# Small matmul groups of the mixers as pieces between contraction blocks: a hybrid pool and HGRN2 layer on one core

## Chip, cores and metric

One core of a Trainium2 chip. The time is that of one execution of the kernel in device microseconds (us); lower is better. Before the change it was run three times.

## What is computed

One layer over 2,048 tokens of width 1,024, in float32, cut to what matters:

```
mod = silu(c) @ ada_w + ada_b                       # shift, scale, gate
h   = rms_norm(x, w_pre) * (1 + scale) + shift
z   = h @ w_in                                      # 1024 -> 6144: u, g (pool), q, f_pre, v, g_h (HGRN2)
pool = trailing mean over 2/4/8/16 tokens minus token, @ pool_w, * scale, * silu(g)
f = lb + (1 - lb) * sigmoid(f_pre);  k = 1 - f      # per head of 128 channels, 8 heads
o_t = q_t @ S_t;  S_t = diag(f_t) S_{t-1} + k_t v_t^T
out = x + gate * rms_norm(concat(pool, rms_norm(o) * silu(g_h)) @ w_out)
```

## The kernel before

The tokens run in two halves of 1,024, each as two blocks of 512 (`BLK`). A **step** is one 2x2 block product by the seven-product scheme of Winograd (`quad`): seven calls of `product` (L351), each four contraction blocks of three 128x512 matmuls (L353, the operands split in a high and a low part), so 84 **products** of 128x512 a step into the three banks `ps_mm`. A head `hd` has three steps: `fq` (forget gate and query), `pool` (one of eight pool columns) and `hv` (gate and value); the list `steps` sets their order. The first half of the tokens has 24 steps and so has the second; then 16 more products, eight for each half of the contraction, make the output projection.

Weights: in the first half `granule` loads a step's columns (`wraw<-w_in`), forms sums on POOL (L324 to L333), splits each of seven operands on ACT (`w<-wraw`, L129) and DVE (L130), and stores them (`wsd<-w`, SP's queue); the second half reads them back.

Beside the products runs the **mixer** of each head, for each block of 512 tokens:

- `attn_unit`: builds the decayed attention of chunks of 128 tokens level by level. `sums` (L574) gives the diagonal and its neighbour; then for m = 2, 4, 8, 16 sixteen matmuls of 32x16 (L614), then those of 32 (L625) and of 64 (L635). After each level `place` copies the result under a mask (DVE, L594) and `update(m)` multiplies the query tile `qk` by a decay (DVE, L606, 128x512). The next level's matmuls read that tile: a chain of six groups with five links for each block and head, 160 links in all.
- `out_unit`: transposes of value and key (L653, L666) with ACT copies `v` and `kd`, outer products `kv` (L671), the chain over four chunks (L679, L681, with DVE's state update L682), squares on ACT (L688), the root on POOL (L111, L112), the scaling on DVE (L690), a transpose (L693), the gate (L694) and a store.

Other side work: `second_sums(i)` (L432 to L457) normalises 128 tokens of the second half, transposes them (L443), writes four tiles `hc` on ACT (L123) and four `hs` on POOL and stores them (`hsd`); `hc` and `hs` have one buffer each. `out_sums` (L712 to L719) loads a part of `w_out` into the tile `x`, scales it on ACT (L713), forms sums on POOL and stores them; `gate_row` makes the output gate.

The code is written step after step and a list scheduler in the framework orders each engine's instructions by a simulated time; what is written earlier has the higher priority. Each engine, and SP's queue, then runs its own list in order. Before the change the main loop wrote a whole step, and behind it the whole mixer part: `attn_unit` of block 0, then of block 1, behind `fq`; `out_unit` of block 0, then of block 1, behind `hv`.

Of the kernel before, what the change touches and what calls it, by code (L numbers as in the profile page):

```python
# [44 lines left out]
def build(nc, tc, a):  # L45
# [6 lines left out]
    with tc.tile_pool(name="dram", bufs=1, space=DRAM) as dram, \  # L52
# [295 lines left out]

        def product(ps, w, s, start):
# [76 lines left out]
        def second_sums(i):  # L426
# [8 lines left out]
            nc.scalar.activation(junk, xt, AF.Square, accum_out=ss)  # L435
            rstd_of(ss, 1, 1.0 / D)
            nc.vector.tensor_scalar(xt, xt, ss, None, ALU.mult)
            for k4 in range(0, KH, 2):
# [5 lines left out]
                for k in range(2):  # L444
# [11 lines left out]
                    for j, t_ in ((0, hc), (4, hs)):  # L456
                        nc.sync.dma_start(hsd[j:j + 4, :, k4 + k, i * n:(i + 1) * n].rearrange("j p t -> p j t"), t_)  # L457

# [9 lines left out]
        def gate_row():  # L468

            gn = wsp.tile([P, D], F32, name="gn", tag="x1", bufs=1)  # L470
            for j in range(KB):
                for n in range(2):
                    ns = slice(n * BLK, (n + 1) * BLK)
                    t_ = short("adag", "junk")
                    nc.sync.dma_start(t_, ada_w[:, j, 2 * D + n * BLK:2 * D + (n + 1) * BLK])
                    if j == 0:
                        nc.vector.tensor_scalar(gn[:, ns], t_, sc[:, 0:1], None, ALU.mult)
                    else:
                        nc.vector.scalar_tensor_tensor(gn[:, ns], t_, sc[:, j:j + 1], gn[:, ns], ALU.mult, ALU.add)
            for n in range(4):  # L480
# [8 lines left out]
                nc.sync.dma_start(gnrow[:, ns], b_)  # L489

# [72 lines left out]
        def attn_unit(hd, b, qk, tm):  # L563
# [18 lines left out]
            sums(w0, 0)  # L582
            nc.vector.tensor_tensor(Q, Q, f, ALU.mult)
            Qp, Kp = (t_.rearrange("p (n two) -> p n two", two=2) for t_ in (Q, K))
            w1 = short("w1", "w0", 2, n=BLK // 2)
            nc.gpsimd.tensor_tensor(w1, Qp[:, :, 1], Kp[:, :, 0], ALU.mult)
            sums(w1, 1)
# [20 lines left out]
            update(1)  # L608
            for m in (2, 4, 8, 16):
# [8 lines left out]
            for q in range(4):  # L618
                qs = slice(q * 32, (q + 1) * 32)
                nc.scalar.copy(attn[qs, :, qs], diag[qs])  # L620
            ps = bank("lv", (P, NC_, 32))
            for c in range(NC_):
                for q in (0, 2):
                    t = c * C + q * 32
                    nc.tensor.matmul(ps[q * 32:(q + 1) * 32, c], K[:, t:t + 32], Q[:, t + 32:t + 64],  # L625
                                     start=True, stop=True)
            for q in (0, 2):
                eng = nc.vector.tensor_copy if q else nc.scalar.copy
                qs = slice(q * 32, (q + 1) * 32)
                eng(attn[qs, :, (q + 1) * 32:(q + 2) * 32], ps[qs])  # L630
            update(32)
            ps = bank("lv", (P, NC_, 64))
            for c in range(NC_):
                t = c * C
                nc.tensor.matmul(ps[0:64, c], K[:, t:t + 64], Q[:, t + 64:t + 128], start=True, stop=True)  # L635
            nc.scalar.copy(attn[0:64, :, 64:128], ps[0:64])
            update(64)
            return attn, qk, tm[C]

        def hv_step(W):  # L640
# [5 lines left out]
            for b in range(2):  # L646
                pre = gx if b else X
                g = short("g", "g", 2, pool=ws)
                nc.scalar.activation(g, pre, AF.Sigmoid)
                nc.vector.tensor_tensor(g, pre, g, ALU.mult)  # L650
                ps = bank("tp", (P, NC_, P))
                for c in range(NC_):
                    nc.tensor.transpose(ps[:, c], vc[b][:, c * C:(c + 1) * C], ident)  # L653
                v = ws.tile([P, NC_, P], F32, name="v", tag="v", bufs=2)
                nc.scalar.copy(v, ps)
                r.append((v, g))
            return r

        def out_unit(hd, t0, attn, qk, td, v, g):

            first = t0 == 0
            Q, K = qk[:, 0], qk[:, 1]

            ps = bank("tp", (P, NC_, P))
            for c in range(NC_):
                nc.tensor.transpose(ps[:, c], K[:, c * C:(c + 1) * C], ident)  # L666
            kd = ws.tile([P, NC_, P], F32, name="kd", tag="kd", bufs=1)
            nc.scalar.copy(kd, ps)
            kv = bank("kv", (P, NC_, P))
            for c in range(NC_):  # L670
                nc.tensor.matmul(kv[:, c], kd[:, c], v[:, c], start=True, stop=True)  # L671
            sx = ws.tile([P, NC_ - 1, P], F32, name="sx", tag="sx", bufs=1)
            st = state[hd]
            ops = bank("o", (P, NC_, P))
            for c in range(NC_):
                s_in = st if c == 0 else sx[:, c - 1]
                s_out = st if c == NC_ - 1 else sx[:, c]
                zero = first and c == 0
                nc.tensor.matmul(ops[:, c], attn[:, c], v[:, c], start=True, stop=zero)  # L679
                if not zero:  # L680
                    nc.tensor.matmul(ops[:, c], Q[:, c * C:(c + 1) * C], s_in, start=False, stop=True)  # L681
                    nc.vector.scalar_tensor_tensor(s_out, s_in, td[:, c:c + 1], kv[:, c], ALU.mult, ALU.add)  # L682
                else:
                    nc.vector.tensor_copy(s_out, kv[:, c])
            og = short("og", "og", 3).rearrange("p (c v) -> p c v", v=P)
            ss = ws.tile([P, NC_], F32, name="ss", tag="ss", bufs=4)
            for c in range(NC_):
                nc.scalar.activation(og[:, c], ops[:, c], AF.Square, accum_out=ss[:, c:c + 1])  # L688
            rstd_of(ss, NC_, 1.0 / P)
            nc.vector.tensor_tensor(og, ops, view(ss, 0, [(1, NC_), (0, P)]), ALU.mult)  # L690
            ps = bank("tp", (P, NC_, P))
            for c in range(NC_):
                nc.tensor.transpose(ps[:, c], og[:, c], ident)  # L693
            nc.vector.tensor_tensor(g, ps.rearrange("p c t -> p (c t)"), g, ALU.mult)  # L694
            store_mix(KB + hd, t0, g)
# [9 lines left out]
        def out_sums(g, k, c):  # L705

            n = 2 * P
            t_ = wsp.tile([P, 4, n], F32, name="x1", tag="x1", bufs=1)
            for h in range(2):
                kb = k + h * KH  # L710
                src = w_out[:, g * KB + kb].rearrange("p (n c) -> p n c", n=2)
                nc.sync.dma_start(t_[:, 2 * h:2 * h + 2], src[:, :, c * n:(c + 1) * n])  # L712
# [101 lines left out]
        for i, step in enumerate(steps):  # L814
# [24 lines left out]
            if half == 1 and what == "hv" and n == 3:  # L839
                gate_row()  # L840
# [67 lines left out]
```

## Time and profile before

| | us |
|---|---|
| three runs | 1807.91 (median), 1806.59, 1812.88 |
| the profiled execution, its own time | 1806.18 |
| its span, first to last instruction | 1804.2 |
| PE busy (matmul) | 1637.2 (91%) |
| DVE / POOL / ACT busy | 1116.9 / 713.4 / 640.4 |
| mean granted clock of TensorE | 0.959 of full speed |
| first product starts | 58.2 |
| first half (from the second step on) | 125.3 to 791.8 |
| second half | 791.8 to 1445.5 |
| output projection | 1445.5 to 1804.2 |

PE's busy time counts from the start to a modelled end of overlapping matmuls; what is lacking to the span is time in which it ran none. The granted clock has two levels, full speed (2.4 GHz) and half (1.2 GHz); a mean of 0.95 in a stretch is a tenth of it at half speed. A wait is put down to the operation that ended last before it.

### The profile page before, as it was taken

To read this page: it belongs to the slowest core of one execution; us is meant where nothing else is said; L and a number is where in the kernel's file an instruction comes from. 1 tells how busy PE (TensorE), PEld (TensorE's weight loads), DVE (VectorE), ACT (ScalarE), POOL (GpSimd) and SP (SyncE) were. 2 spreads that over 40 slices of the span, in tenths; PEclk is the share of its full clock that TensorE was granted. 3 is DMA by queue.
4 is the path that set the end of the run, shared out by engine and by line. 5 is a ranking of instruction groups with operands and counts; after the bars stand their busy time and mean duration, and the time that the engine had idled before them with its cause. 6 is when DMAs were issued, how large, how long until landed. Compare 5 with 4: busy or idle time off the path is not lost.

```text
span 1804.2 us, 31567 instructions
## 1 busy us (share of the span) xinstructions
PE 1637.2 (91%) x12249; PEld 1294.7 (72%) x12249; DVE 1116.9 (62%) x1763; ACT 640.4 (35%) x1409; POOL 713.4 (40%) x915
## 2 busy tenths in 40 slices
PE   7779899998999699899998999989999889998897
PEld 6557677776777477677787787767787668876675
DVE  5496676676667465777445434444454775486886
ACT  4654243434343434342222222232221432252332
POOL 1374454647262727513212213444221323225664
PEclk8789999999999799899999999989999999999999
DMA  9646565767475647796442545657555552364554
GB/s 344 222 134 211 181 205 182 227 197 240 167 228 193 196 145 244 228 360 222 149 157 86 189 160 199 197 189 241 181 164 174 199 186 106 116 218 167 189 189 148
DMA packets 221475, 348.66 MB, mean 193 GB/s; under 512 B 45009, under 2 KB 152590, under 8 KB 221326
## 3 DMA queue, kind: packets, MB, share of 16 engines
q1 hardware_dynamic: 221240, 346.62, 57.5%
q8 instruction: 97, 1.59, 0.4%
q14 instruction: 52, 0.43, 0.1%
q10 hardware_dynamic: 86, 0.03, 0.0%
HBM read 203.99 MB, written 142.61 MB: 192 GB/s over the span
## 4 chain that ended last, share of the span: by engine, by line
PE 41%; DMA 16%; DVE 15%; POOL 12%; issue 9%; ACT 6%; SPq 1%; POOLq 0%; DVEq 0%; ACTq 0%
PE ps_mm L353 33%; DMA wraw<-w_in 3%; DMA x<-w_out 3%; DVE m L130 2%; DVE w L130 2%; DMA wos<-x 2%; PE ps_lv L614 1%; DVE lo L130 1%; DVE qk L606 1%; ACT w L129 1%; POOL wraw L324 1%; PE ps_o L681 1%; DVE y L884 1%; POOL wraw L327 1%; DMA wraw<-wup 1%
## 5 line engine op out<-in xcount | busy, mean ns | idle before, releaser
L353 PE MATMUL ps_mm<-hi,w 128*128 128x512 f32 x2304 | 786.0, 410 | 39.0 <-ACT ue L371 5.4
L353 PEld LDWEIGHTS ps_mm<-hi,w 128*128 128x128 f32 x2304 | 444.0, 194 | 146.3 <-ACT ue L371 6.5
L353 PE MATMUL ps_mm<-lo,w 128*128 128x512 f32 x1152 | 466.2, 405 | 12.5 <-DVE lo L130 9.4
L353 PE MATMUL ps_mm<-hi,m 128*128 128x512 f32 x896 | 286.2, 398 | 32.4 <-DVE y L380 9.2
L353 PEld LDWEIGHTS ps_mm<-lo,w 128*128 128x128 f32 x1152 | 223.3, 194 | 59.6 <-DVE lo L130 12.4
L353 PEld LDWEIGHTS ps_mm<-hi,m 128*128 128x128 f32 x896 | 170.2, 191 | 79.6 <-ACT m L129 10.6
L130 DVE TENSOR_TENSOR w<-wraw,w 128x512 fp32r<-128x512 f32 x168 | 140.5, 844 | 107.2 <-ACT w L129 91.5
L606 DVE TENSOR_TENSOR qk<-qk,tcn 128x512 f32<-128x512 f32 x192 | 153.0, 797 | 61.2 <-PE ps_lv L635 39.8
L129 ACT CAST w<-wraw 128x512 fp32r<-128x512 f32 x168 | 101.9, 620 | 212.8 <-DMA wraw<-w_in 65.2
L353 PE MATMUL ps_mm<-lo,m 128*128 128x512 f32 x448 | 177.0, 395 | 0.0
L353 PE MATMUL ps_mm<-hi,wpair 128*128 128x512 f32 x384 | 132.0, 404 | 4.0 <-DVE sg L504 3.6
L111 POOL TENSOR_SCALAR ss<-ss 128x4 f32<-128x4 f32 (+2 forms) x60 | 19.9, 331 | 223.2 <-ACT og L688 131.9
L353 PEld LDWEIGHTS ps_mm<-lo,m 128*128 128x128 f32 x448 | 85.5, 191 | 17.4
L614 PEld LDWEIGHTS ps_lv<-qk 128*32 128x32 f32 x4096 | 49.8, 113 | 53.9 <-issue 39.7
L353 PEld LDWEIGHTS ps_mm<-hi,wpair 128*128 128x128 f32 x384 | 73.0, 191 | 19.9 <-DVE sg L504 3.7
L614 PE MATMUL ps_lv<-qk 128*32 128x16 f32 x4096 | 64.2, 186 | 17.6 <-DVE qk L606 17.5
L324 POOL TENSOR_TENSOR wraw<-wraw 128x512 f32<-128x512 f32 x24 | 33.3, 1388 | 110.3 <-DMA wraw<-w_in 43.8
L594 DVE COPY_PREDICATED diag<-mask,ps_lv 128x64 f32<-128x64 uint8 x128 | 31.0, 242 | 74.1 <-PE ps_lv L614 73.0
L353 PE MATMUL ps_mm<-lo,wpair 128*128 128x512 f32 x192 | 76.1, 397 | 0.0
L130 DVE TENSOR_TENSOR m<-mraw,m 128x512 fp32r<-128x512 f32 x64 | 62.0, 976 | 19.9 <-ACT m L129 19.9
L130 DVE TENSOR_TENSOR m<-S,m 128x512 fp32r<-128x512 f32 x48 | 44.1, 918 | 42.8 <-ACT m L129 41.9
L557 POOL TENSOR_TENSOR tcn<-tcn 128x128 f32<-128x128 f32 (+4 forms) x160 | 67.0, 419 | 8.9
(277 smaller groups left out, 2602.8 us busy)
## 6 DMA issues: line engine op xcount, KB each, us to landing
wsd<-w SPq DMA_DIRECT2D x168, 512.0 KB
w<-wsd SPq DMA_DIRECT2D x120, 512.0 KB
wpair<-wsd SPq DMA_DIRECT2D x24, 1024.0 KB
wraw<-w_in SPq DMA_DIRECT2D x40, 512.0 KB
mraw<-mix SPq DMA_DIRECT2D x32, 512.0 KB
ada<-ada_w SPq DMA_DIRECT2D x16, 512.0 KB
mix<-g SPq DMA_DIRECT2D x32, 256.0 KB
mix<-sg SPq DMA_DIRECT2D x32, 256.0 KB
```

Of the source, the lines that this page charges most:

```text
L111: nc.gpsimd.tensor_scalar(ss, ss, inv, EPS, ALU.mult, ALU.add)
L129: nc.scalar.copy(hi, raw)
L130: nc.vector.tensor_tensor(lo, raw, hi.bitcast(F32), ALU.subtract)
L324: nc.gpsimd.tensor_tensor(B11, B12, B11, ALU.subtract)
L327: nc.gpsimd.tensor_tensor(B11, B22, B11, ALU.subtract)
L353: nc.tensor.matmul(ps, w[:, a_, k], s[k][b_], start=start and k == a_ == b_ == 0, stop=k == KH - 1 and a_ == 1, skip_group_check=not start)
L557: nc.gpsimd.tensor_tensor(dst, sv[:, :, 0], sv[:, :, 1], ALU.mult)
L594: nc.vector.copy_predicated(dst, mk, view(data, 0, [(16, NC_), (m, n), (1, m)]))
L606: nc.vector.tensor_tensor(dst, dst, t_, ALU.mult)
L614: nc.tensor.matmul(ps[q * 32:(q + 1) * 32, c * 16:(c + 1) * 16], K[:, t:t + 32], view(Q, t + m, [(2 * m, 16 // m), (1, m)]), start=True, s ...
L681: nc.tensor.matmul(ops[:, c], Q[:, c * C:(c + 1) * C], s_in, start=False, stop=True)
L884: nc.vector.scalar_tensor_tensor(y[t][:, ns], y[t][:, ns], ss, gn[:, ns], ALU.mult, ALU.mult)
```

## The change

`product` calls `tick()` before each of its four contraction blocks, 28 times a step. A list `side` holds closures; `tick` runs the next ones at a pace that empties the list within a step, and `drain` runs the rest when the step has been written.

```diff
+        side = []
+        pace = [0.0, 1.0]
+        def beside(groups, delay=0):
+            side.extend([lambda: None] * delay + groups)
+            pace[:] = [0.0, (len(side) + 1) / 27]
+        def tick():
+            pace[0] += pace[1]
+            while pace[0] >= 1 and side:
+                pace[0] -= 1
+                side.pop(0)()
...
             for k in range(KH):
+                tick()
                 for a_, b_ in ((0, 0), (0, 1), (1, 0)):
```

`attn_unit` now returns eight pieces instead of running: the diagonal, the neighbour, levels 2, 4, 8, 16, 32 and 64 (`same`, `neighbour`, `level`, `level32`, `level64`). The main loop alternates the pieces of the two blocks and lays them beside the step that follows `fq`. `out_unit` returns five pieces (turn the key, turn the value, `outer`, `chunks`, `gated`), and `out_units` interleaves those of two blocks with empty places. The value's transposes move from `hv_step` into these pieces; the tile `kd` gets two buffers.

```diff
-            return attn, qk, tm[C]
+            return [same, neighbour, *(lambda m=m: level(m) for m in (2, 4, 8, 16)), level32, level64]
...
-            kd = ws.tile([P, NC_, P], F32, name="kd", tag="kd", bufs=1)
+            kd = ws.tile([P, NC_, P], F32, name="kd", tag="kd", bufs=2)
...
+            no = lambda: None
+            return [k0, v0, k1, o0, v1, c0, no, o1, no, g0, c1, no, no, no, g1]
...
             if what == "fq":
                 fq = fq_step(n, W, None if i else second_block)
                 nxt = nxt or weights(steps[1])
-                pending = [attn_unit(n, b, *fq[b]) for b in range(2)]
+                drain()
+                beside(mixed([attn_unit(n, b, *fq[b]) for b in range(2)]), 2)
             elif what == "hv":
                 vg = hv_step(W)
-                for b in range(2):
-                    out_unit(n, base + b * BLK, *pending[b], *vg[b])
+                drain()
+                beside(out_units(n, base, fq, vg))
             else:
                 pool_step(n, base, W)
-            if half == 0 and what == "hv" and n < HEADS - 2:
-                second_sums(n)
-            if half == 0 and what == "pool" and n in (2, 4):
-                second_sums(HEADS - 4 + n // 2 + 1)
-            if half == 1 and what == "hv":
-                out_sums(0, n % 4, n // 4)
-            if half == 1 and what == "hv" and n == 3:
-                gate_row()
+                drain()
```

The other side work becomes pieces too. `second_sums(n)` stands beside every head's `hv` step, one for each head, the last beside the last pool step (before, it was six times behind `hv`, and twice more behind pool steps 2 and 4). `gate_row` is split over the second half's `hv` steps 2 and 3, `out_sums` into load, scaling and sums with empty places between, two of them beside each `hv` step from the fourth head on.

```diff
+            if half == 0 and (what == "hv" and n < HEADS - 1 or what == "pool" and n == HEADS - 1):
+                beside(second_sums(n), 2)
+            if half == 1 and what == "hv" and n in (2, 3):
+                row = gate_row() if n == 2 else row[10:]
+                beside(row[:10])
+            if half == 1 and what == "hv" and n >= 4:
+                beside(out_sums(0, n - 4, 0) + out_sums(0, n - 4, 1))
...
-            if half == 1 and what == "hv" and n == HEADS - 1:
+            if half == 1 and what == "pool" and n == HEADS - 2:
                 ws_cm.__exit__(None, None, None)
```

In the second half the pool step now stands ahead of its head's `hv` step, as in the first. The work itself, the shapes and the numbers of instructions are the same; new line numbers are L610 (sums), L655, L669, L681 (levels), L636 (place), L648 (update), L466 (transposes of `second_sums`), L373 (products).

Three places of the built order. PE, first half, around the mixer of the seventh head, before (`ps_lv<-qk` are level matmuls, `x_5505` the tokens of a `second_sums`):

```order
L353 MATMUL ps_mm<-hi,w 128x512
L614 MATMUL ps_lv<-qk 32x16 x48
L443 MATMUL ps_tp<-ident,x_5505 128x128 x4
L625 MATMUL ps_lv<-qk 32x32 x8
L635 MATMUL ps_lv<-qk 64x64 x4
L653 MATMUL ps_tp<-ident,vc 128x128 x4
L353 MATMUL ps_mm<-hi,w 128x512
L353 MATMUL ps_mm<-lo,w 128x512
```

Three levels of one block (48 matmuls), the level of 32 and that of 64 stand behind one another without a product between.

PE, first half, the seventh head now:

```order
L373 MATMUL ps_mm<-hi,w 128x512
L466 MATMUL ps_tp<-ident,x_6326 128x128
L373 MATMUL ps_mm<-hi,w 128x512
L373 MATMUL ps_mm<-lo,w 128x512
L373 MATMUL ps_mm<-hi,w 128x512
L655 MATMUL ps_lv<-qk 32x16 x16
L669 MATMUL ps_lv<-qk 32x32 x8
L373 MATMUL ps_mm<-hi,w 128x512
L373 MATMUL ps_mm<-lo,w 128x512
```

The level of 16 of one block and the level of 32 of the other stand together, and 21 products follow before the next pair (L669 and L681).

DVE, first half, the seventh head now, from the update of block 0 to that of block 1 behind the level of 8 (`diag_138` is block 1's, `s_` the pool's window sums):

```order
L648 TENSOR_TENSOR qk<-qk,tcn 128x2x32x8
L406 TENSOR_TENSOR gx<-ps_mm,gx 128x512
L130 TENSOR_TENSOR w<-wraw,w 128x512
L549 TENSOR_TENSOR s_6283<-s__6281 128x524
L559 SCALAR_TENSOR_TENSOR s_6271<-s_6271,ue 128x512
L130 TENSOR_TENSOR w<-wraw,w 128x512
L554 TENSOR_TENSOR s_6285<-s_6283 128x520
L540 TENSOR_TENSOR sg<-gx,sg 128x512
L560 TENSOR_TENSOR sg<-sg,s_6271 128x512
L559 SCALAR_TENSOR_TENSOR s_6285<-s_6285,ue 128x512
L636 COPY_PREDICATED diag_138<-mask_192,ps_lv 128x8x8
L648 TENSOR_TENSOR qk<-qk,tcn 128x2x32x8
```

The first `qk` is block 0's, the last block 1's: between the updates of the two blocks at one level lie nine operations of the pool step and of the split of the next weights.

## Rows read from the trace of the kernel before

**Rows 1.** Windows by stage: length, busy PE PEld DVE ACT POOL, PEclk, DMA, GB/s.
```profile
125.30:791.80 666.50, 610.85 (x5179) 478.56 (x5178) 455.27 (x726) 267.09 (x616) 338.02 (x444) 0.95 0.64 211
791.80:1445.50 653.70, 619.39 (x5357) 492.24 (x5355) 331.94 (x606) 186.92 (x468) 177.90 (x262) 0.99 0.55 184
1445.50:1804.20 358.70, 318.35 (x1344) 254.15 (x1344) 247.90 (x313) 118.56 (x208) 148.60 (x122) 0.97 0.48 164
```

**Rows 2.** Lines by form, PE, first half: count, busy, mean ns, idle before.
```profile
L353 PE MATMUL ps_mm<-hi,w 128*128 128x512 f32 x1281 | 435.0, 410 | 15.5 <-DVE sg L504 3.0 <-ACT vc L371 2.7 <-DVE g L650 2.5
```

**Rows 3.** Waits of PE, first half: us in total, times, longest.
```profile
PE ps_lv L614 <- DVE qk L606: 13.9, 6, 3.7
PE ps_tp L653 <- ACT hc L123: 11.0, 4, 6.7
PE ps_kv L671 <- ACT kd L668: 4.8, 4, 1.9
...
PE ps_tp L693 <- DVE og L690: 2.7, 2, 2.1
```

**Rows 4.** Lines by form, PE, second half.
```profile
L353 PE MATMUL ps_mm<-hi,w 128*128 128x512 f32 x960 | 323.7, 402 | 15.8 <-ACT ue L371 4.7 <-ACT gx L361 4.3 <-DVE sg L504 1.8
...
L353 PE MATMUL ps_mm<-hi,wpair 128*128 128x512 f32 x376 | 129.3, 405 | 4.0 <-DVE sg L504 3.6 <-DVE gx L386 0.2 <-DVE f L386 0.2
```

**Rows 5.** Timeline of PE at 610 us: start, us, instruction, idle before.
```profile
610.34 0.45 PE L614 MATMUL ps_lv<-qk 128*32 128x16 f32 x32 [1.65 <-DVE qk L606]
614.52 0.63 PE L614 MATMUL ps_lv<-qk 128*32 128x16 f32 x32 [3.74 <-DVE qk L606]
...
627.38 1.11 PE L653 MATMUL ps_tp<-ident,vc 128*128 128x128 f32 x4 [6.67 <-ACT hc L123]
629.17 0.79 PE L353 MATMUL ps_mm<-hi,w 128*128 128x512 f32 x1 [0.68 <-ACT ue L371]
```

**Rows 6.** Timeline of DVE in the same stretch.
```profile
609.50 0.69 DVE L606 TENSOR_TENSOR qk<-qk,tcn 128x512 f32<-128x512 f32 x1
612.00 1.64 DVE L130 TENSOR_TENSOR w<-wraw,w 128x512 fp32r<-128x512 f32 x1 [1.81 <-ACT w L129]
...
613.69 0.68 DVE L606 TENSOR_TENSOR qk<-qk,tcn 128x512 f32<-128x512 f32 x1
```

**Rows 7.** Timeline of ACT in the same stretch.
```profile
621.34 0.81 ACT L123 ACTIVATE hc<-ps_tp,sh,af 128x128 f32<-128x128 f32 x2 [4.28 <-DMA hsd<-hc]
```

**Rows 8.** Windows of a head each, and of a stretch at half clock.
```profile
319.70:400.20 80.50, 79.30 (x672) 61.33 (x672) 57.54 (x94) 33.59 (x80) 43.36 (x61) 1.00 0.66 213
571.60:674.50 102.90, 83.72 (x704) 65.87 (x703) 57.22 (x98) 39.03 (x93) 48.38 (x74) 0.87 0.57 181
986.10:1056.10 70.00, 69.97 (x556) 55.96 (x555) 27.99 (x51) 17.36 (x46) 14.48 (x26) 1.00 0.52 172
...
611.20:635.10 23.90, 10.48 (x80) 8.08 (x81) 6.09 (x9) 6.28 (x13) 11.01 (x22) 0.50 0.43 122
```

**Rows 9.** Waits of ACT, 1090 to 1260 us.
```profile
ACT x L713 <- DMA x<-w_out: 89.1, 13, 13.8
```

**Rows 10.** Timeline of PE at 689 us, back-to-back products.
```profile
689.27 0.39 PE L353 MATMUL ps_mm<-lo,w 128*128 128x512 f32 x1
...
689.95 0.39 PE L353 MATMUL ps_mm<-lo,w 128*128 128x512 f32 x1
```

**Rows 11.** Lines of DVE, first half: count, busy, mean ns, idle before.
```profile
L130 DVE TENSOR_TENSOR w<-wraw,w 128x512 fp32r<-128x512 f32 x159 | 132.6, 841 | 102.5 <-ACT w L129 86.9 <-PE ps_mm L353 5.9 <-POOL x L718 3.3
L606 DVE TENSOR_TENSOR qk<-qk,tcn 128x512 f32<-128x512 f32 x96 | 81.6, 850 | 12.7 <-PE ps_lv L635 8.3 <-PE ps_lv L625 4.4
L594 DVE COPY_PREDICATED diag<-mask,ps_lv 128x64 f32<-128x64 uint8 x64 | 15.3, 240 | 11.4 <-PE ps_lv L614 10.9
```

**Rows 12.** Lines of DVE, second half.
```profile
L606 DVE TENSOR_TENSOR qk<-qk,tcn 128x512 f32<-128x512 f32 x96 | 71.4, 744 | 48.4 <-PE ps_lv L635 31.5 <-PE ps_lv L625 16.9
```

**Rows 13.** Timeline of POOL in the stretch of rows 5.
```profile
611.84 1.25 POOL L326 TENSOR_TENSOR wraw<-wraw 128x512 f32<-128x512 f32 x1
```

More of the change, by code (lines that the diff above doesn't have):

```diff
@@ L489, in gate_row @@
                 nc.sync.dma_start(gnrow[:, ns], b_)
+            fetch(0, 0)
+            return [lambda i=i: add(i // 2, i % 2) for i in range(2 * KB)] + [lambda i=i: total(i) for i in range(4)]
         def store_mix(kb, t0, src):
@@ L606, in update, with level @@
                 nc.vector.tensor_tensor(dst, dst, t_, ALU.mult)
-            update(1)
-            for m in (2, 4, 8, 16):
+            def level(m):
                 ps = bank("lv", (P, NC_ * 16))
@@ L650, in hv_step, with out_unit, turn @@
                 nc.vector.tensor_tensor(g, pre, g, ALU.mult)
+                r.append((vc[b], g))
+            return r
+        def out_unit(hd, t0, b, qk, tm, vc, g):
+            first = t0 == 0
+            Q, K = qk[:, 0], qk[:, 1]
+            attn, td = accs[b][0], tm[C]
+            kd = ws.tile([P, NC_, P], F32, name="kd", tag="kd", bufs=2)
+            v = ws.tile([P, NC_, P], F32, name="v", tag="v", bufs=2)
+            og = short("og", "og", 3).rearrange("p (c v) -> p c v", v=P)
+            kv = []
+            def turn(dst, src):
@@ new lines, in gated, with out_units @@
+            def gated():
+                ps = bank("tp", (P, NC_, P))
+                for c in range(NC_):
+                    nc.tensor.transpose(ps[:, c], og[:, c], ident)
+                nc.vector.tensor_tensor(g, ps.rearrange("p c t -> p (c t)"), g, ALU.mult)
+                store_mix(KB + hd, t0, g)
+            return (lambda: turn(kd, K)), (lambda: turn(v, vc)), outer, chunks, gated
+        def out_units(hd, base, fq, vg):
+            (k0, v0, o0, c0, g0), (k1, v1, o1, c1, g1) = (
+                out_unit(hd, base + b * BLK, b, *fq[b], *vg[b]) for b in range(2))
+            no = lambda: None
+            return [k0, v0, k1, o0, v1, c0, no, o1, no, g0, c1, no, no, no, g1]
@@ L778, in build @@
                 steps.append((half, "fq", hd))
-                if half == 0 and hd >= 1:
-                    steps.append((half, "pool", hd - 1))
+                behind = hd - 1 - half
+                if behind >= 0:
+                    steps.append((half, "pool", behind))
                 if half == 0 and hd == HEADS - 1:
@@ L783, in build @@
                 steps.append((half, "hv", hd))
-                if half == 1 and hd >= 2:
-                    steps.append((half, "pool", hd - 2))
             steps += [] if half == 0 else [(half, "pool", KB - 2), (half, "pool", KB - 1)]
@@ L811, in second_block, with mixed @@
             first_sums()
-        pending = []
+        def mixed(units):
+            return [f for pair in zip(*units) for f in pair]
+        heads = None
         for i, step in enumerate(steps):
@@ L865, in build @@
             if g == 0:
-                out_sums(1, p_ % 4, p_ // 4)
+                for f in out_sums(1, p_ % 4, p_ // 4):
+                    f()
                 for t in range(2):
```

191 lines of the change are left out of this document (102 added, 89 removed).

## The prediction

> **What bounds the kernel now.** First the windows by stage [rows 1]: PE ran matmuls for 610.9 of 666.5 us in the first half and for 619.4 of 653.7 in the second, with DVE at 455 and 332, and DMA at 0.64 and 0.55. So PE sets the pace of both halves, and what can be won is what it lacks: 55.7 us idle in the first half, 34.3 in the second, and the time at half clock. The granted clock of 0.95 means a tenth of 666.5, about 67 us, at half speed; 0.99 means about 13 us. The output projection has 40.4 us idle, but the change moves nothing in it.
>
> Second, who ends the idle time. Of the first half's 55.7 us the products themselves waited 15.5 [rows 2]; the other 40.2 stand before small groups: 13.9 before level matmuls on the update of the query tile, 11.0 before the value's transposes, 4.8 before the outer products, 2.7 before the output's transposes, the rest in waits of 2 us or less [rows 3]. In the second half products waited 15.8 + 4.0 [rows 4], small groups about 14.
>
> Third, one such place. At 610 us levels stand without products between (first order fence of the change): the second waits 1.65, the third 3.74 us, the value's transposes 6.67 [rows 5]. An update alone takes 0.69 us, but DVE's list held a weight split of 1.64 us, itself late by 1.81, ahead of the next [rows 6]. The 6.67 us are another thing: ACT stood before `hc` for 4.28 us until the store of the earlier `hc` had landed [rows 7], with two `second_sums` one behind the other. The clock then fell: 611.2 to 635.1 ran at half, with PE busy 10.5 of 23.9 us [rows 8].
>
> Fourth, what a head costs without such places: 80.5 us in the first half (PE idle 1.2), 70.0 in the second, against 102.9 for the worst shown [rows 8].
>
> **The change, part by part.** *Levels.* I counted in the built orders what PE has between the end of one level and the next of the same block, a product at 0.227 us (three in 0.68 [rows 10]), small matmuls by their spacing in the trace. A link needs about 1.5 us: update 0.69 [rows 6], the masked copy before it (0.24 [rows 11]), the level itself and the hand-over. Before, 21 of 160 links have less than 1.5 us, 33 less than 3 (62 us short of 3 in sum). Now none has less than 1.5, three slightly less than 3, 103 have 5 to 6. The same count for output units: six outer products stood too near their transposes, now none; seven output transposes less than 4 us behind the last chunk, now two.
>
> *`second_sums`.* Eight before and after. Before, the transposes of two of them stood 40 and 43 products apart at two places; now at least 187 lie between any two. The wait for the one-buffer `hc` within one `second_sums` stays.
>
> These two own the 40.2 us. I leave 4 (the near links that remain, one `hc` wait of about 4.3 [rows 7]): **minus 36**. The bounds are 0 and 40. In the second half, 14 go to 2: **minus 12**.
>
> *Clock.* 67 us at half clock, of which 24 are the stretch of rows 8 with 10.5 of work; taking the other 43 at 80% busy, 45 us of work ran at half, and 22 would be saved at full. The falls I looked at follow waits, but short ones follow clusters of small groups that remain; I take half of it, **minus 12**, and **minus 4** of at most 6 in the second half.
>
> *`out_sums` in pieces.* ACT stood 89 us before the scaling until `w_out` had landed, up to 13.8 at a time [rows 9], and products of the second half waited 4.7 and 4.3 on ACT [rows 4]. Load and scaling are now apart as written, but the tile still has one buffer. **Minus 3**, bounds 0 and 9.
>
> *Denser clusters that count as busy*, where small groups follow one another at their own latency: **minus 4**, bounds 0 and 10.
>
> *DVE, against it.* In the first half the mixer's levels of both blocks now lie in one stretch of about 154 products a head (mean of eight; 202 before). For the fourth head the new DVE list there holds 17 weight splits at 0.841, 14 updates at 0.850, 12 masked copies at 0.240 [rows 11] and 38 others: 28 whole 128x512 operations, set at the 0.69 of rows 6, and ten small ones, set at half of it. 14.3 + 11.9 + 2.9 + 22.8 = 52 us. PE has 149 products there, 33.8 us, and most of the 23 us of small work that a smooth head holds (80.5 less 252 products at 0.227 [rows 8, 10]), some 18: 52 too. So DVE is full in that stretch, where before 60 us met 73. DVE also loses time in its list: 102.5 us of 666.5 before weight splits [rows 11]. At that rate the stretch would be 8 us too long a head, 64 in all; the other bound is 0, since the smooth head had DVE at 57.5 of 80.5 and hardly a wait [rows 8]. Nearer to the smooth head: 1.5 us a head, **plus 12**. What is late then is the update, and behind it on DVE the addition that frees a product's bank.
>
> *Half boundary.* The last `second_sums` moves from 276 products ahead of the boundary to 97, 22 us and its small work. Behind its last transposes come two `hc` pairs (0.81 each [rows 7]), a landing (4.3) and then store, load and split of the operands, which I set at 10: some 16. It fits, but SP's queue stands between: **plus 3**, bounds 0 and 10.
>
> *At nothing:* the value's transposes that move, the second `kd` buffer, the later release of the pool `ws`, the second half's pool step ahead of `hv`. They issue the same instructions, and PE's products cover them (two heads have at most 0.2 and 1.2 us idle [rows 8]). Without that cover a turn with its ACT copy costs about 1 us, 64 of them. Start and projection: nothing, give or take 6.
>
> The sum is -36 - 12 - 12 - 4 - 3 - 4 + 12 + 3 = **-56**. The profiled execution took 1806.2 (2.0 around its span), so 1750.2; the median of the three runs is 1.7 above it: **1752 us**.
>
> **Rivals.** *Every head at the smooth pace.* 23 steps at 80.5/3 are 617 (minus 49), the second half loses its 34 idle and 4 of clock: -87, 1721 us. For it: heads of 70.0 and 80.5 exist. Against it: products wait on their own 15.5 and 20 us, and DVE fills up.
>
> *The first half gives most of it back.* With 4.5 us a head for DVE, 36 in place of 12: 1776 us. For it: the 102.5 us of waiting before splits.
>
> *Nothing moves.* Both orders come from the same scheduler's simulated times, and the chip's lateness may only come up elsewhere: waits leave the levels and return before products. Then 1808. Against it: 33 near links become three.
>
> *Slower: updates held up by POOL.* Beside a POOL sum of 1.25 us [rows 13] a split took 1.64 us where an update alone took 0.69 [rows 6]; the mean update is 850 ns in the first half and 744 in the second [rows 11, 12], where POOL is busy half as long [rows 1]. The mean says that 17% of the first half's updates are hit: (850 - 690)/950. An update now holds both blocks, and the levels have no other time to move to. With 31 updates and splits a head in the stretch at 0.95 us, a share of about half costs 9.5 us a head more than now, 76 in all in place of 12: 1816. It turns slower from 8.5 us a head. The Trainium skill, "SBUF — State Buffer", section "Who interferes with whom", has a rule that speaks against this change: a DVE instruction with two inputs in SBUF and a GpSimd instruction that reads SBUF lock each other out for the whole instruction. By that rule the 1.64 us are a full wait behind POOL, and every such meeting in the full stretch lands on the chain. Rows 6 show it of one split, but the update at 613.69, 0.68 us, went through at once [rows 6]: who comes first decides, and POOL's work is the same as before.
>
> **How the numbers follow.** The forecast 0.50 (1735 to 1768 by itself), smooth pace 0.17, given back 0.14, nothing 0.06, slower 0.13. A change of 0.3%, some 5 us, is about what a measurement of this kernel can tell. So faster 0.81, same 0.06, slower 0.13. The range 1715 to 1800 takes in the forecast, the case given back and nearly all of the smooth pace, and leaves out nothing moved and slower.
>
> **What would show it.** Right: hardly any idle time of PE before level matmuls; no stretch like 611 to 635; the granted clock near 0.99 in both halves; the second half near 630 us, the first near 630. Wrong: idle time of 40 us or more before products in the first half with DVE as releaser, DVE above 80% there, or updates whose mean has risen well above 850 ns; a wait of over 10 us at the half boundary before the first product's operands.

## The result and the profile after

The median fell from 1807.3 us (four runs, 1806.2 to 1812.9) to **1726.2 us** (four runs, 1723.9 to 1729.6): ratio 0.9547, 95% interval 0.9521 to 0.9573. That is 81 us less, where 56 were forecast.

The windows by stage of the kernel after (bounds are the first products of the stages; columns as in [rows 1]):

```profile
123.80:718.20 594.40, 574.31 (x5179) 462.45 (x5178) 432.86 (x716) 254.21 (x599) 322.22 (x426) 0.99 0.68 225
718.20:1363.80 645.60, 614.93 (x5351) 492.19 (x5350) 336.45 (x610) 190.68 (x474) 173.68 (x280) 0.98 0.58 193
1363.80:1723.30 359.50, 321.89 (x1345) 254.78 (x1343) 250.72 (x319) 124.70 (x218) 148.23 (x120) 0.97 0.50 171
```

Against [rows 1] the first half is 72.1 us shorter, the second only 8.1, the projection 0.8 longer; the start gave 1.5. In the first half PE's idle time fell from 55.7 to 20.1 us and its busy time from 610.9 to 574.3. In the second half idle went from 34.3 to 30.7, busy from 619.4 to 614.9.

PE's lines by form in the first half (count, busy, mean ns, idle before), beside [rows 2]:

```profile
L373 PE MATMUL ps_mm<-hi,w 128*128 128x512 f32 x1285 | 418.7, 400 | 6.7 <-DVE vc L395 3.8 <-ACT ue L391 1.7 <-DVE qk L400 0.8
...
L655 PE MATMUL ps_lv<-qk 128*32 128x16 f32 x2048 | 27.8, 185 | 0.8 <-DVE diag L636 0.5 <-DVE qk L648 0.3
```

PE's waits in the first half (us, times, longest), beside [rows 3]:

```profile
PE ps_tp L745 <- DVE og L740: 7.1, 6, 2.1
...
PE ps_tp L466 <- ACT hc L123: 1.4, 2, 0.9
...
PE ps_lv L655 <- DVE qk L648: 0.3, 1, 0.3
```

Levels (now L655) wait 0.3 us on the update (L648) where they waited 13.9, the value's transposes no longer wait on `hc` (11.0 before), and even the products wait 6.7 in place of 15.5. The largest wait left is that of the output's transposes on `og`, 7.1 of 20.1 us. A stretch like 611 to 635 us [rows 8] is gone: the trace's clock records hold 61.4 us at half clock in the first half before and 6.8 after. In the second half they hold 17.1 before and 23.9 after.

Two places of the second half held back its gain. The first is its first step, here after the change and then before it:

```profile
718.20:759.20 41.00, 31.80 (x147) 24.62 (x146) 24.92 (x43) 18.89 (x46) 6.19 (x12) 0.92 0.78 264
```

```profile
791.80:815.60 23.80, 23.80 (x127) 20.16 (x126) 14.49 (x24) 13.05 (x29) 5.66 (x9) 1.00 0.88 311
```

Before, the step took 23.8 us without idle time. The timelines of PE, then of ACT, in that step of the kernel after:

```profile
743.62 0.50 PE L373 MATMUL ps_mm<-hi,w 128*128 128x512 f32 x1 [2.19 <-ACT hi L129]
...
749.05 0.56 PE L373 MATMUL ps_mm<-hi,w 128*128 128x512 f32 x1 [1.46 <-ACT hi L129]
```

```profile
742.95 2.39 ACT L129 CAST hi<-sum 128x512 fp32r<-128x512 f32 x4 [5.17 <-DMA sum<-hsd]
748.38 1.14 ACT L129 CAST hi<-sum 128x512 fp32r<-128x512 f32 x2 [3.05 <-DMA sum<-hsd]
```

A product waits for the cast of its operand, and the cast for the load of the sums. Such waits are 5.4 us of the step's 9.2 us of idle time; 3.6 us stand before the output's transposes. The last store of `hsd` was issued 83 us ahead of the boundary before and 11 us ahead after; the last load of sums 21 us behind the boundary before, 39 behind it after.

The second place is the six steps from `hv` of the fifth head to `pool` 4, where `out_sums` now runs. (It runs from the fifth head on, not from the fourth as the description of the change has it: `n >= 4` counts from 0.) The window of the kernel after, then ACT's longest wait between 1065 and 1190 us:

```profile
1044.10:1214.90 170.80, 154.91 (x1289) 122.72 (x1288) 75.94 (x135) 51.27 (x121) 69.56 (x106) 0.96 0.69 227
```

```profile
ACT x L781 <- DMA x<-w_out: 76.1, 17, 9.5
```

15.9 us of these 170.8 PE is idle, while ACT stands before the scaling of `w_out` much as before [rows 9]. In the kernel before, the six steps from `hv` of the fifth head to `fq` of the seventh (1082.3 to 1262.2) took 179.9 us with 16.6 idle. So this place lost nothing against the kernel before; runs 1, 5 and 6 show that it could have gained more.

### The profile page after: what moved, and what is told of

The parts are those of the page before. It is cut to its first block, busy times and chain, and to the rows that moved or that the text cites. A ratio compares the mean times of both kernels' runs of the same rounds, so it can differ in the third digit from the quotient of the medians.

```text
span 1723.3 us, 31604 instructions
## 1 busy us (share of the span) xinstructions
PE 1599.1 (93%) x12249; PEld 1278.4 (74%) x12249; DVE 1101.9 (64%) x1763; ACT 638.3 (37%) x1409; POOL 694.5 (40%) x915
## 4 chain that ended last, share of the span: by engine, by line
PE 47%; DMA 17%; DVE 12%; POOL 10%; issue 7%; ACT 4%; SPq 1%; POOLq 0%; DVEq 0%; ACTq 0%
PE ps_mm L373 38%; DMA x<-w_out 4%; DMA wraw<-w_in 3%; DMA wos<-x 3%; DVE m L130 2%; DVE w L130 2%; PE ps_lv L655 2%; DVE lo L130 2%; DMA wraw<-wup 1%; POOL wraw L324 1%; DMA ada<-ada_w 1%; PE ps_tp L714 1%; PE ps_o L730 1%; DVE y L961 1%; PE ps_o L732 1%
## 5 line engine op out<-in xcount | busy, mean ns | idle before, releaser
L373 PE MATMUL ps_mm<-hi,w 128*128 128x512 f32 x2304 | 764.6, 404 | 21.7 <-ACT hi L129 5.8
L373 PEld LDWEIGHTS ps_mm<-hi,w 128*128 128x128 f32 x2304 | 437.4, 192 | 119.9 <-ACT hi L129 8.5
L373 PE MATMUL ps_mm<-lo,w 128*128 128x512 f32 x1152 | 463.8, 403 | 13.9 <-DVE lo L130 10.7
L373 PE MATMUL ps_mm<-hi,m 128*128 128x512 f32 x896 | 289.2, 401 | 27.4 <-DVE y L400 9.8
L373 PEld LDWEIGHTS ps_mm<-lo,w 128*128 128x128 f32 x1152 | 220.8, 192 | 64.2 <-DVE lo L130 15.4
L373 PEld LDWEIGHTS ps_mm<-hi,m 128*128 128x128 f32 x896 | 171.3, 192 | 75.8 <-DVE y L400 11.0
L373 PE MATMUL ps_mm<-lo,m 128*128 128x512 f32 x448 | 177.9, 397 | 3.5 <-DVE lo L812 3.5
L648 DVE TENSOR_TENSOR qk<-qk,tcn 128x512 f32<-128x512 f32 x192 | 152.8, 804 | 14.9 <-PE ps_lv L669 9.7
L373 PE MATMUL ps_mm<-hi,wpair 128*128 128x512 f32 x384 | 131.6, 402 | 0.8 <-DVE gx L406 0.8
L373 PEld LDWEIGHTS ps_mm<-lo,m 128*128 128x128 f32 x448 | 86.0, 192 | 22.4 <-DVE lo L812 4.2
L111 POOL TENSOR_SCALAR ss<-ss 128x4 f32<-128x4 f32 (+2 forms) x60 | 16.1, 269 | 182.9 <-ACT og L738 81.5
L373 PEld LDWEIGHTS ps_mm<-hi,wpair 128*128 128x128 f32 x384 | 73.0, 191 | 17.7 <-issue 1.6
L373 PE MATMUL ps_mm<-lo,wpair 128*128 128x512 f32 x192 | 76.7, 399 | 0.1
L834 POOL TENSOR_TENSOR S<-mraw 128x512 f32<-128x512 f32 x16 | 24.3, 1516 | 117.8 <-DMA mraw<-mix 113.5
L130 DVE TENSOR_TENSOR m<-mraw,m 128x512 fp32r<-128x512 f32 x64 | 62.8, 988 | 12.9 <-ACT m L129 12.9
L655 PEld LDWEIGHTS ps_lv<-qk 128*32 128x32 f32 x4096 | 45.5, 111 | 31.1 <-issue 23.5
L392 POOL TENSOR_TENSOR vc<-vc,gx 128x512 f32<-128x512 f32 x16 | 24.4, 1525 | 101.6 <-ACT vc L391 101.6
```

What stands on the lines that cost most here:

```text
L130: nc.vector.tensor_tensor(lo, raw, hi.bitcast(F32), ALU.subtract)
L392: nc.gpsimd.tensor_tensor(c22, c22, c21, ALU.add)
L648: nc.vector.tensor_tensor(dst, dst, t_, ALU.mult)
L655: nc.tensor.matmul(ps[q * 32:(q + 1) * 32, c * 16:(c + 1) * 16], K[:, t:t + 32], view(Q, t + m, [(2 * m, 16 // m), (1, m)]), start=True, s ...
L834: nc.gpsimd.tensor_tensor(S1, A21, A22, ALU.add)
```

## Experiments

All kernels are edits of the changed kernel, and each ratio is to the kernel before, run on the same chip. On the chips of these runs the kernel before took 1805 to 1810 us in the median, so that times of different runs compare to within some 5 us. Windows are those of one profiled execution, which lies up to 9 us from the median of its run.

**1. Mixers' pieces alone.** Side work back whole and at its old steps:

```diff
-            if half == 0 and (what == "hv" and n < HEADS - 1 or what == "pool" and n == HEADS - 1):
-                beside(second_sums(n), 2)
...
+            if half == 0 and what == "hv" and n < HEADS - 2:
+                for f in second_sums(n):
+                    f()
```

and `out_sums`, `gate_row` likewise.

> The changed kernel with the side work put back: second_sums, gate_row and out_sums whole and at the steps where the kernel before has them; the mixers' pieces, alternating, stay. In the built order 7 level links are nearer than 1.5 us and 13 nearer than 3 (19 us short of 3 in sum; 0, 3 and 0 with the change, 21, 33 and 62 before). Theory 1 (both parts count: waits before small groups come from near links, made by the mixers and by two second_sums close together, and the clock follows them): the value's transposes wait for hc again (some 11 us), a few levels wait, the clock falls again in one or two places: first half about 615, total about 1748 us. Rival (it is the spread side work that brings the gain, pieces of mixers are neutral): first half 650 or more, total 1785 or more. Rival (mixers alone bring it): 1730 or less.

Measured: 1726.4 us, ratio 0.956 (0.954 to 0.958): as fast as the whole change. Windows of its two halves:

```profile
125.40:752.10 626.70, 588.87 (x5180) 470.52 (x5178) 454.88 (x737) 265.21 (x615) 334.38 (x442) 0.98 0.69 229
752.10:1369.70 617.60, 605.32 (x5354) 487.24 (x5352) 322.25 (x589) 180.81 (x457) 164.18 (x264) 0.99 0.56 185
```

Theory 1 fell for the total, which is the one that the rival "mixers alone" gave (1730 or less). The first half is 626.7 (theory 1 said 615), 32 us longer than with spread side work, but not by its reason: the value's transposes wait only 0.4 us for `hc`, not 11. The second half is 28 shorter, 617.6 to 645.6. In total the spread side work is worth nothing beside the mixers' pieces.

**2. Side work alone.** The pieces called at once, block after block (`for f in attn_unit(...): f()`, and the same for `out_units`).

> The changed kernel with the mixers' groups issued in one go behind fq and hv, block 0 whole and then block 1, as before; only the side work is spread. 7 links nearer than 1.5 us, 23 nearer than 3 (24 us short in sum). Theory 1: no wait for hc and fewer near links than before, but dense clusters of small groups as before, so busy time hardly falls: first half about 635, total about 1770 us. Rival (the spread side work brings it all): first half about 600, total 1735 or less. Rival (side work is neutral): 1800.

Measured: 1775.8 us, ratio 0.983 (0.980 to 0.986), near theory 1's 1770. Its "busy time hardly falls" did not hold: that of the first half fell by 14.1 us.

```profile
121.70:752.70 631.00, 596.75 (x5175) 468.40 (x5174) 447.42 (x720) 258.62 (x602) 330.79 (x426) 0.98 0.64 213
752.70:1414.40 661.70, 626.46 (x5357) 496.79 (x5355) 337.92 (x607) 182.33 (x462) 181.14 (x280) 0.98 0.55 184
```

With [rows 1] and run 1 this splits the halves. First half: mixers alone -39.8, side work alone -35.5, both -72.1, so they nearly add. Second half: mixers alone -36.1, side work alone **+8.0**, both -8.1, so there they do not. Both runs keep the new step order of the second half: the +8.0 is of side work and step order together, and no run parts the two.

**3. Blocks not alternating.**

```diff
-                beside(mixed([attn_unit(n, b, *fq[b]) for b in range(2)]), 2)
+                beside([f for b in range(2) for f in attn_unit(n, b, *fq[b])], 2)
```

> The changed kernel with the attention groups of block 0 all ahead of those of block 1 in the list of pieces, where the change alternates them; nothing else. 21 links nearer than 1.5 us, 34 nearer than 3 (59 us short in sum): as before the change. Theory 1 (distance between the levels of a block is what counts): some 20 us of idle time before levels in the first half and some 10 in the second, the clock at half for another 20 to 30 us: total about 1765 us. Rival (DVE works the same updates in the same time whichever block they belong to, so alternation is worth nothing): 1726 to 1731.

Measured: 1793.9 us, ratio 0.994 (0.992 to 0.996). 68 of the 81 us are lost. PE's waits in its first half are spread over many places (51.6 us idle in all), the longest groups:

```profile
PE ps_tp L466 <- ACT hc L123: 6.4, 4, 2.7
PE ps_lv L681 <- DVE qk L648: 4.9, 5, 1.8
PE ps_mm L373 <- DVE vc L395: 4.4, 3, 2.8
PE ps_mm L373 <- ACT w L129: 4.4, 4, 2.4
```

The rival is out: DVE does the same updates, but a block's next level has half the distance. Theory 1 named the direction and undersized it (1765): products and transposes wait too, not levels alone.

**4. Later `second_sums` one step earlier.**

```diff
-            if half == 0 and (what == "hv" and n < HEADS - 1 or what == "pool" and n == HEADS - 1):
-                beside(second_sums(n), 2)
+            if half == 0 and what == "hv" and n < HEADS - 1:
+                for i_ in ([n], [n], [2, 3], [4], [5], [6], [7])[n]:
+                    beside(second_sums(i_), 2)
```

> The changed kernel with the eight second_sums one step of a head earlier from the fourth on (two of them beside hv of head 2), so that the last is beside hv of head 6 and not beside the last pool step. Theory 1 (the first step of the second half took 41.0 us, with 9.0 idle and three falls of the clock, because the last hsd store landed at about 709 us and the loads and splits of the sums then came late): that step falls to about 26, total about 1714 us. Rival (the loads of the sums are held by SP's queue behind other loads and the buffers, whenever the stores are done): the step stays near 40, total 1722 to 1728.

Measured: 1715.4 us, ratio 0.951 (0.949 to 0.953). The first step of the second half:

```profile
731.30:757.00 25.70, 25.70 (x145) 22.18 (x144) 17.03 (x32) 15.17 (x37) 4.93 (x10) 1.00 0.73 267
```

25.7 in place of 41.0 us, no idle time, the clock full: the late sums made that wait. The rival is out. The first half pays 11.0 of it back (605.4), with 3.6 us idle beside the two `second_sums` that now stand close. Of the 10.8 us in total, 5 lie in the projection (354.5 to 359.5), which the edit does not touch.

**5. Scaling of `w_out` on POOL.** `nc.scalar.activation(...)` in `scale` becomes `nc.gpsimd.tensor_scalar(..., out_scale(...), None, ALU.mult)`.

> The changed kernel with the scaling of w_out in out_sums(0, ...) and out_sums(1, ...) issued on POOL instead of ACT; nothing else. With the change ACT stood 76 us (17 times) before this scaling between 1065 and 1190 us until w_out had landed, and the steps there hold some 14 us of idle PE. Theory 2 (the pieces of out_sums, now in four heads instead of eight, hold up ACT's list, and behind it the mixers' and products' copies): most of it goes, total about 1716 us. Rival (those waits are the mixers' own, or POOL behind the load holds up the same chains): 1722 to 1735.

Measured: 1710.7 us, ratio 0.947 (0.945 to 0.950). The six steps, then what now stands before the scaling:

```profile
1042.00:1195.00 153.00, 148.07 (x1322) 118.75 (x1321) 76.09 (x136) 36.33 (x96) 92.28 (x112) 1.00 0.70 228
```

```profile
POOL x L781 <- DMA x<-w_out: 62.1, 13, 8.2
```

153.0 in place of 170.8 us and 4.9 idle in place of 15.9. POOL waits for the load as ACT did, but PE waits only 1.4 us for POOL there. Theory 2 holds for this place: what stood behind the scaling in ACT's list was held up. The edit also takes the scaling's own work off ACT (busy 51.3 to 36.3 us in the six steps), and the run does not part that from the wait.

**6. `out_sums` and `gate_row` as before the change**, `second_sums` spread.

> The changed kernel with gate_row and out_sums put back as before the change (whole, one out_sums behind each hv of the second half, gate_row behind the fourth); second_sums stays spread. Theory 2 (second half slowed by out_sums in four heads): the second half falls from 645.6 to about 635, total about 1716 us. Rival (the fast second half of the run with mixers alone, 617.6, came from its half boundary alone, which stays late here): second half 645, total 1722 to 1730.

Measured: 1724.5 us, ratio 0.955 (0.952 to 0.957), the rival's number, yet not by its reason: the six steps fell to 157.9 us, as theory 2 has it, while the four steps behind the boundary rose from 121.4 to 132.8, the first of them from 41.0 to 45.8. The trace shows the loads of `out_sums` in SP's queue among the late loads of the sums there; that they cause the rise is not shown.

**7. The same, with the last `second_sums` one step earlier** (`what == "pool" and n == HEADS - 2`).

> The kernel of the run before in this series, with only the last second_sums moved from the last pool step of the first half to the one ahead of it (in the built order its last transposes move from 97 products ahead of the boundary to 145). Theory 2: the first step of the second half falls from 41 to about 27 us and the first half stays at 595 to 600: total about 1703 us. Rival (what is won at the boundary is lost in the first half, as 11 us were with all later sums moved): 1712 or more.

Measured: 1710.4 us, ratio 0.948 (0.946 to 0.950), 14 less than run 6, between the two. The boundary step is 38.1 us (45.8 in run 6), not 27: the last transposes stand 48 products earlier, and the last load of sums still comes 38.5 us behind the boundary; in run 4 it comes 15.3 behind it.

**8. More work for DVE.** Ahead of each update of the first half:

```diff
+                    for i_ in range(2):
+                        nc.vector.tensor_tensor(scr, K[:, i_ * 256:(i_ + 1) * 256], K[:, i_ * 256:(i_ + 1) * 256], ALU.mult)
```

> The changed kernel with two more multiplications of 128x256 on DVE (about 0.35 us each, into a tile that nobody reads) ahead of each update of the first half: some 10 us a head, 78 us in all. Theory (DVE had 44 us of work in 56 in the mixers' stretch, not 52 in 52 as the prediction had it, so there is room for most of it): 1726 to 1750 us. Rival (the stretch is as full as the prediction had it, and the updates pass what is added on to the levels): 1785 or more.

Measured: 1748.9 us, ratio 0.969 (0.966 to 0.973). DVE's added line and the window of the first half:

```profile
L646 DVE TENSOR_TENSOR scr<-qk 128x256 f32<-128x256 f32 x222 | 127.7, 575 | 5.5 <-ACT qk L583 3.8
```

```profile
125.70:748.40 622.70, 587.88 (x5180) 471.53 (x5178) 539.96 (x938) 255.32 (x599) 336.64 (x424) 0.97 0.65 214
```

The durations of what was added sum to 128 us, not 78, DVE's busy time rose by 107 (432.9 to 540.0), and the first half became 28 longer: some 80 us found room. DVE was not full.

**9. The second half's pool step behind `hv`, as before.** The line `behind = hd - 1 - half` and its test give way to the two tests of the old list.

> The changed kernel with the pool step of the second half put back behind hv (order fq, hv, pool of two heads back, as before the change); nothing else. The pieces of attention then share the seven products of hv with the side work and are emitted several at a time: 25 level links nearer than 1.5 us and 68 us short of 3 in sum, all in the second half (0 and 0 with the change). Theory 3 (the step order is what gives the levels room in the second half): second half 25 us or more longer, total about 1755 us. Rival (the prediction: this move is worth nothing): 1722 to 1730.

Measured: 1763.4 us, ratio 0.974 (0.972 to 0.977). Its second half, and the two longest of PE's waits there:

```profile
718.80:1409.70 690.90, 625.24 (x5352) 502.98 (x5350) 341.16 (x617) 197.00 (x485) 182.16 (x278) 0.95 0.55 185
```

```profile
PE ps_lv L681 <- DVE attn L674: 15.8, 5, 9.9
PE ps_tp L714 <- ACT kd L715: 11.7, 7, 7.3
```

45.3 us longer than with the change, and 37 longer even than before it. The step order is not neutral. Without a pool step behind `fq`, the pieces of attention and the side work share the 84 products of one `hv` step, and the level of 64 and the turns of the output units wait longest. How the loss divides between them is not shown.

**10. Output units in one go**, attention in pieces: `for f in out_units(...): f()`, in the old order.

> The changed kernel with the output units issued in one go behind hv (value transposes of both blocks, then block 0 whole, then block 1), as before the change; the attention pieces and the side work stay. 2 outer products stand too near their transposes (6 before, 0 with the change), 6 output transposes nearer than 4 us to the last chunk (7, 2), 3 level links nearer than 1.5 us. Theory 1 (each near link costs its shortfall): 10 to 20 us, total about 1741 us. Rival (output units are short and ACT and DVE have time for them: worth nothing): 1722 to 1730. Rival (they are half of the gain, as they are half of the small groups): 1760 or more.

Measured: 1745.2 us, ratio 0.965 (0.962 to 0.968): the pieces of the output units are worth 19 us, within theory 1's 10 to 20. Its two halves:

```profile
122.30:746.70 624.40, 591.63 (x5176) 473.41 (x5175) 436.64 (x715) 255.03 (x598) 318.95 (x427) 0.98 0.65 214
746.70:1384.10 637.40, 615.65 (x5356) 492.75 (x5354) 333.46 (x610) 185.54 (x467) 180.13 (x280) 0.99 0.58 192
```

Against the change the first half is 30.0 us longer and the second 8.2 shorter: in these executions the pieces of the output units pay in the first half alone.

**11 and 12. Two versions that beat both kernels.** Run 11 joins run 5 with `second_sums` in the order `[0, 1], [2], [3], ...`, run 12 joins runs 4 and 5.

> The changed kernel with two edits: the scaling in out_sums on POOL (15.6 us less in the run with that alone), and two second_sums beside hv of the first head, then one a head, so that the last is beside hv of head 6. If the half boundary and the waits of ACT for w_out are the two places where the change gives time back, and they add up: first step of the second half about 26 us, first half 594 to 600, total about 1696 us. Rival (two second_sums close together cost the first half what the boundary gains, as with 11 us in the earlier move): 1705 or more.

> The changed kernel with the two edits that gained by themselves: second_sums one step earlier from the fourth on (10.8 us less by itself) and the scaling in out_sums on POOL (15.6 us less by itself). If the late half boundary and ACT's waits for w_out are two separate places, they add up: 1726.2 - 10.8 - 15.6, about 1700 us, with a first half of 605 and a second of about 610. Rival (the two share their gain, since both leave ACT and SP freer in the second half): 1706 to 1712, as in the run with two second_sums beside the first hv.

Measured: 1708.1 us, ratio 0.944 (0.942 to 0.946), and 1705.3 us, ratio 0.944 (0.942 to 0.946). Both lie below the change's interval. Of the 26 us that the two edits gained alone, run 12 keeps 21: it lands a little under its rival's 1706 to 1712, so part of the gain is shared. Run 11 shows the rival's way: its boundary step is 25.8 us, its first half 611 where 594 to 600 was hoped.

## Why the prediction was right, and by how much not

Faster, the range and the mechanism held; the gain was undersized by a third (81 us, 56 forecast). By halves, the terms of the first sum to -40 where -72 was measured, those of the second to -16 where it was -8: what the second half fell short hides part of what the first gained beyond the forecast. By its terms:

- **Level waits and `second_sums`, first half: minus 36, measured minus 26.8.** The idle time before small groups fell from 40.2 to 13.4, not to 4; the output's transposes alone wait 7.1 on `og` (2.7 before). Another 8.8 came from the products' own waits (15.5 to 6.7), which the prediction left as they were. That the whole fall of idle time, 35.6, meets the term is luck. Mixers and side work both count: with mixers alone 37.8 us stay idle, with side work alone 34.3. Run 3 bears out the count of near links, which put that kernel beside the one before, but its price, the shortfall of a link, is too small.
- **Clock, first half: minus 12, measured about minus 17 to minus 20.** The 67 us were read from a rounded 0.95; of the 61.4 us at half clock that the records hold, 45.9 were work, and 6.8 us are left, all of them work. At twice the pace that is 20 us saved, at the pace of products in the trace (436 ns each at half clock, 240 at full) 17. The prediction took half of such a sum, on the reason that falls behind clusters of small groups would stay. But ahead of each of the ten falls before stand waits of PE, 1.6 to 2.2 us in sum, and none follows a cluster of small groups without one; eight of the ten went with the waits.
- **Denser clusters: minus 4, bounds 0 and 10, measured about minus 17 to minus 20.** That is what the fall of 36.5 us in busy time leaves beside the clock. It lies outside the bounds: at full clock a product is 238 ns behind the last in place of 240.5, some 5 us over 1,930, and the small groups take 12 to 15 less.
- **DVE, against it: plus 12, bounds 0 and 64, measured nothing in sum.** This is the term that failed most. The stretch was said to hold 52 us of DVE in 52 of PE. The trace shows less. The first line here runs from the first to the last level matmul of the fourth head, which are the 149 products that the forecast counted; the second holds two whole steps, the pool step of the fourth head and `hv` of the fifth:

```profile
331.90:381.00 49.10, 49.10 (x553) 40.03 (x552) 39.10 (x73) 20.90 (x55) 26.44 (x33) 1.00 0.68 223
```

```profile
404.80:460.50 55.70, 54.18 (x562) 43.39 (x560) 43.87 (x79) 21.73 (x58) 28.94 (x35) 0.97 0.61 208
```

  DVE is busy for 39.1 of 49.1 us in the one and for 43.9 of 55.7 in the other, and in the first PE is never idle. The 81 operations of the forecast are about those of two whole steps (79), so they lie beside 168 products, not 149. And durations overlap: the 79 sum to some 49 us, but back to back one of 0.68 us starts every 0.60 (last section), which takes 5 us off. Over the whole first half DVE is at 73%, below the 80% named as the sign of failure, and PE's waits on DVE fell from 30.6 to 14.1 us. Run 8 then added 107 us of busy time for 28 us of time.
- **Half boundary: plus 3, bounds 0 and 10, measured plus 15 to 17** (41.0, against 25.7 in run 4 and 23.8 before). The 16 us behind the last transposes were too few: the chain of loads, casts and splits of the seven operands starts late and stays late to its last load. Run 4 removes the delay; what keeps the chain late once it has begun is not shown.
- **Second half: minus 12 and minus 4.** With the change itself idle time fell by 3.6 only, and the time at half clock rose by 6.8. The mixers' pieces alone gave minus 36.1 there (run 1), idle time 34.3 to 12.3 and busy time 14 less, more than both terms. With the change the boundary and `out_sums` took most of that back, run 1 against the change: 15.2 in the first step, 10.3 in the six steps.
- **`out_sums` in pieces: minus 3, bounds 0 and 9. The sign was wrong**: with it back at its old places the six steps are 10.3 (run 1) and 12.9 us (run 6) shorter. The prediction saw the one buffer and ACT's wait, and not that the same work now falls in four heads instead of eight. Run 5 gives the price of having the scaling on ACT: 15.6 us.
- **"At nothing", the pool step ahead of `hv`:** wrong by 37 us of the total (run 9). It was costed by the instructions that it issues; its worth is the room that it gives to other pieces. The second half's gain rested on it unsaid.

Of the rivals, 1721 us at the smooth pace comes nearest in time, but not as it reasoned: the first half is 594, below its 617, and the second 646. The fourth head, the smooth one of [rows 8], now takes 74.5 us (308.6 to 383.1) against its 80.5.

**Held up by POOL** did not decide, though its mechanism is there. I paired each decay update (`qk<-qk,tcn`, L648, L606 before) of both halves with POOL's instructions in the trace. Before the change 97 of 192 ran beside one, 904 ns in the mean and up to 1,833; the others took 687. After, 69 did, at 1,017 ns, and the others took 685. So the delay is about 21 us of DVE before and 23 after. In the first half alone the mean update did rise, from 850 to 895 ns, a mild form of the sign that the prediction named: 52 of 96 met POOL (61 before), and the delay went from 15.7 to 20.5 us. The Trainium skill, "SBUF — State Buffer", section "Who interferes with whom", says that a DVE instruction with two SBUF inputs contends with a GpSimd instruction that reads SBUF, under an exclusive lock. The longest updates agree with it; but of the 97 meetings before, half lasted 691 ns or less, so a meeting need not cost anything. The rival's time (1816) did not come, since fewer updates meet POOL and DVE had room for the delay.

What stays open: how much of the change's gain in busy time is clock and how much density, which is split here by the clock records and not by a run; how the +8.0 of run 2 divides between side work and step order; and whether the boundary could be freed without the 11 us in the first half.

## What to carry to other kernels

When small dependent groups fill in between large products, count for each chain how much other work lies between two links, and make room by alternating independent chains and by the order of the steps: here alternation was worth 68 us and the place of the pool steps 37. Spread side work by what the engine that runs it would wait for and by when its result is due: a load waited for on ACT, or a result needed at the next stage, can take back much of what even spacing gains. A resource's share in a stretch is to be summed from the real forms of its instructions, not from one whole-tile price.

## What the runs showed of the hardware

The added multiplications of run 8, two SBUF inputs of 128x256, took 414 ns where no POOL instruction overlapped (85 of 224, at most 426) and 672 in the mean beside one (139, up to 1,527). The same view of that line:

```profile
L646 DVE TENSOR_TENSOR scr<-qk x224: 405/418/1527, 113.1 to 729.5; 128x256 f32<-128x256 f32 x112
```

So nearly all of the spread belongs to meetings with POOL.

And durations of DVE instructions can't be added up. Its timeline in the kernel after, at 709 us:

```profile
708.65 0.68 DVE L559 SCALAR_TENSOR_TENSOR s<-s,ue 128x512 f32<-128x512 f32 x1
709.25 0.68 DVE L697 TENSOR_TENSOR g<-ps_mm,g 128x512 f32<-128x512 f32 x1
709.85 0.67 DVE L395 TENSOR_TENSOR vc<-ps_mm,gx 128x512 f32<-128x512 f32 x1
```

Each lasts 0.67 or 0.68 us and the next starts after 0.60. Of the 1,763 DVE instructions 1,125 begin before the one ahead has ended, by 81 ns in the median, 95 us in all.
